# In a seven-product pair the low part of the loaded blocks is made behind the fourth sum

## The chip, the cores and the metric

The kernel runs on one core of a Trainium2 chip. The metric is the device time of one execution in microseconds; the median of three runs of the kernel before is 911.48 us (911.47 to 912.15). The engines are called as the profile calls them: PE (matmul) with PEld (its weight loads), DVE (vector), ACT (scalar), POOL, and SP, whose queue issues the loads.

## The reference

One layer of a decoder trunk on 256 tokens of width 2048, cut to what matters here:

```python
h = rmsnorm(x, norm_g)
h, gate = adaln(h, c, ada_w, ada_b)
proj = jnp.einsum('bsd,de->bse', h, w_in)          # 2048 -> 4 * 4096
b_gate, c_gate, v, g = jnp.split(proj, 4, axis=-1)
u = causal_depthwise_conv(c_gate * v, conv_w)
y = b_gate * u * jax.nn.silu(g)
y = jnp.einsum('bse,ed->bsd', y, w_out)            # 4096 -> 2048
x = x + gate[:, None, :] * y
return rmsnorm(x, final_g)
```

The change lies in the second product, `y` (256 x 4096) by `w_out` (4096 x 2048).

## The kernel before

**Numbers in two parts.** All products are of fp32 numbers, which PE multiplies in a reduced form. So each operand is split: a high part, a cast to `fp32r` on ACT, and a low part, the operand minus its high part, on DVE. A product then is three matmuls (`triple`): high by high, high by low, low by high.

**The stages.** First the norm and the modulation, then the first product, one half of the channels in four chunks and the other in eight pairs of channel tiles (matmuls of line 471, up to about 730 us), then the second product: the first 1024 output columns at once (731 to 816 us), and the other 1024 in two stages of 512 (816 to 903 us). All of its matmuls are line 695.

**The stage of the change** walks through 16 pairs of channel tiles in the order `0, 1, 10, 2, 11, 3, 12, 4, 13, 5, 14, 6, 15, 7, 8, 9`. For each pair the SP queue loads a 1 MiB block of `w_out` (`raw_o`, line 684), 128 partitions by four blocks of 512: two rows of tiles by two halves of columns. An ordinary pair casts it (ACT, line 341, `hi<-raw_o`), takes its low part (DVE, line 346, `lo<-raw_o`) and makes 2 x 2 x 2 products of three matmuls, 24 matmuls, into the PSUM tiles `wide` (`mm_w`).

Pairs 10 to 15 are pairs of seven products: with sums of the token tiles (`forms`, the profile's `form`, made in the stage before) and sums of the blocks of `w_out`, seven products take the place of eight, 21 matmuls in place of 24. From the middle of the stage ordinary pairs and these take turns, and one of each is called a round below. In `seven` the four loaded blocks are `b[:, 0]` to `b[:, 3]`:

- line 720, DVE: the first and the second sum, `b1 - b0` and `b2 - b0` (`sums_o`)
- line 721, ACT: the high part of blocks 1 to 3 (`hi<-raw_o`, 128x1536)
- line 722, DVE: the third sum, block 2 plus the first sum
- line 723, DVE: the fourth sum, block 3 minus the third sum
- line 724, DVE: the low part of blocks 1 to 3
- line 725: the high part (ACT, line 341, `hi<-sums_o`) and the low part (DVE, line 346, `lo<-sums_o`) of the four sums together

Then follow the products: lines 730 to 732 by blocks 1, 3 and 2 as loaded, and lines 733 to 736 by the four sums. The first of these products goes into the PSUM tile `p1`; it, `p6` and `p75` are the profile's `mm`.

**Buffers.** There are three buffers of each kind. A round uses the three `lo` buffers for the ordinary load, the load of the pair of seven and the sums, so the load of the next pair of seven goes into the buffer of the last one, as soon as the last reader of that block is done. The three `hi` buffers hold the three high parts of a round: the cast of the next ordinary block waits until PE has used the last one.

**Order.** Each engine runs its queue in order. What order the instructions of a queue have is worked out when the program is built, from the dependences between them and from durations that the builder assumes; it need not be that of the source. `tc.add_manual_dep(a, b, after, ...)` adds a dependence without a wait: on the same engine, `a` comes behind `b` in the queue. In the trace of before, line 724 stands in front of line 722 in five of the six pairs (DVE: 720, 724, 722, 723), and between 722 and 723 in the pair at 746 us.

Of the kernel before, what the change touches and what calls it, by code (L numbers as in the profile page):

```python
# [8 lines left out]
F32 = mybir.dt.float32  # L9
F32R = mybir.dt.float32r  # L10
AF = mybir.ActivationFunctionType
ALU = mybir.AluOpType
# [105 lines left out]
def short_conv_layer(ctx: ExitStack, tc: tile.TileContext, x, c, norm_g, ada_w, ada_b, w_in, conv_w, w_out, final_g, out):  # L118
    nc = tc.nc
# [25 lines left out]
    def w_tile(kind, name, dtype=F32, i=None):  # L145

        if i is None:
            i = nth[kind] % 3
            nth[kind] += 1
        return wpool.tile([P, SLOT], dtype, tag=f"{kind}{i}", name=name, bufs=1)  # L150
# [12 lines left out]
    after = mybir.DependencyInfo(mybir.DependencyClass.NoSync, mybir.DependencyReason.DATA)  # L163
# [111 lines left out]
    for t in range(TT):  # L275
        for dh in range(2):
# [3 lines left out]
            else:  # L280
                nc.vector.scalar_tensor_tensor(
                    out=junk[:, t], in0=xt[t][dh], scalar=1.0, in1=xt[t][dh], op0=ALU.mult, op1=ALU.mult,
# [50 lines left out]
    def hi_tile():  # L333
        return w_tile("hi", "hi", F32R)

    def lo_tile(lo_tag="lo"):
        return w_tile(lo_tag, "lo", F32R)
# [23 lines left out]
    def split(raw, n, lo_tag="lo"):  # L361

        return split_lo(raw, n, split_hi(raw, n), lo_tag)
# [64 lines left out]
    sums = {}  # L428
# [139 lines left out]
    def gate(dc):  # L568
        return gates[dc // 2][:, dc % 2, :]
# [119 lines left out]
    def y_parts(ct, t):  # L689
        return [ys[ct // 2][:, ct % 2, h, t * P : (t + 1) * P] for h in range(2)]  # L690

    def triple(dst, y, hi, lo, opens=False, ends=False):

        for i, (a, b) in enumerate(((0, hi), (0, lo), (1, hi))):
            nc.tensor.matmul(dst, y[a], b, start=opens and i == 0, stop=ends and i == 2, skip_group_check=True)  # L695
# [17 lines left out]
    def seven(j, raw):  # L713


        opens, last = j == SEVEN[0], j == SEVEN[-1]
        sums = w_tile("lo", "sums_o")
        hi, lo = hi_tile(), lo_tile("raw")
        b, s, bh, bl = (v.rearrange("p (b f) -> p b f", f=W) for v in (raw, sums, hi, lo))
        nc.vector.tensor_tensor(out=s[:, 0:2], in0=b[:, 1:3], in1=b[:, 0:1].to_broadcast([P, 2, W]), op=ALU.subtract)  # L720
        nc.scalar.copy(bh[:, 1:4], b[:, 1:4])
        nc.vector.tensor_tensor(out=s[:, 2], in0=b[:, 2], in1=s[:, 0], op=ALU.add)
        nc.vector.tensor_tensor(out=s[:, 3], in0=b[:, 3], in1=s[:, 2], op=ALU.subtract)
        nc.vector.tensor_tensor(out=bl[:, 1:4], in0=b[:, 1:4], in1=bh[:, 1:4].bitcast(F32), op=ALU.subtract)
        sh, sl = (v.rearrange("p (b f) -> p b f", f=W) for v in split(sums, SLOT, "raw"))

        def f(i):
            return [forms[j][h][:, i] for h in range(2)]

        triple(p1, y_parts(2 * j, 0), bh[:, 1], bl[:, 1], opens, last)  # L730
        triple(wide[0][:, 1], y_parts(2 * j + 1, 0), bh[:, 3], bl[:, 3])
        triple(wide[0][:, 0], f(3), bh[:, 2], bl[:, 2])
        triple(p75[:, 0], f(2), sh[:, 1], sl[:, 1], opens, last)
        triple(p75[:, 1], f(0), sh[:, 0], sl[:, 0], opens, last)
        triple(p6, f(1), sh[:, 2], sl[:, 2], opens, last)
        triple(wide[1][:, 1], y_parts(2 * j + 1, 1), sh[:, 3], sl[:, 3])
# [12 lines left out]
    for n, j in enumerate(order):  # L749
        raw = w_tile("lo" if n else "raw", "raw_o")  # L750
        load_o(raw, 2 * j, 2, 0, 2 * W)
        load_ends(n - 4)
        if j in SEVEN:
            seven(j, raw)
            if j == SEVEN[-1]:
                gather()
            continue
        hi, lo = split(raw, SLOT, "raw")
        for t in range(TT):
            for k in range(2):  # L760
                for d in range(2):
                    o = slice((k * 2 + d) * W, (k * 2 + d + 1) * W)
                    triple(
                        wide[t][:, d], y_parts(2 * j + k, t), hi[:, o], lo[:, o],
                        n == 0 and k == 0, j == order[-1] and k == 1,
                    )
# [24 lines left out]
    for dc in range(2, 4):  # L791
# [16 lines left out]
        for ep in range(n_ep):  # L808
# [3 lines left out]
            if dc == 3:  # L812
# [3 lines left out]
                    out=raw3, in0=raw3, in1=gate(dc).unsqueeze(1).to_broadcast([P, EP, W]), op=ALU.mult  # L816
# [45 lines left out]
```

## Time and profile before

| | us |
|---|---|
| median of three runs | 911.48 |
| the profiled execution | 911.95 |
| its span | 910.2 |
| PE busy | 894.2 |
| DVE busy | 653.5 |
| ACT busy | 476.1 |
| the six DVE instructions of line 724, together | 10.5 |

The 1.75 us between the profiled execution and its span lie around the span. A group or a timeline row reads: engine, line, operation, `out<-in` by the program's names, shapes, count; in square brackets stands how long the engine was idle before it and what ended that. PE runs matmuls back to back, so that a row of a matmul is longer than the distance to the next one; distances are what counts. A weight load (PEld) carries the wait of its matmul.

### The profile page before, as it was taken

To read this page: it belongs to the slowest core of one execution; us is meant where nothing else is said; L and a number is where in the kernel's file an instruction comes from. 1 tells how busy PE (TensorE), PEld (TensorE's weight loads), DVE (VectorE), ACT (ScalarE), POOL (GpSimd) and SP (SyncE) were. 2 spreads that over 40 slices of the span, in tenths; PEclk is the share of its full clock that TensorE was granted. 3 is DMA by queue.
4 is the path that set the end of the run, shared out by engine and by line. 5 is a ranking of instruction groups with operands and counts; after the bars stand their busy time and mean duration, and the time that the engine had idled before them with its cause. 6 is when DMAs were issued, how large, how long until landed. Compare 5 with 4: busy or idle time off the path is not lost.

```text
span 910.2 us, 16272 instructions
## 1 busy us (share of the span) xinstructions
PE 894.2 (98%) x7029; PEld 854.7 (94%) x7029; DVE 653.5 (72%) x647; ACT 476.1 (52%) x422; POOL 0.7 (0%) x6
## 2 busy tenths in 40 slices
PE   6999999999999999999999999999999999999996
PEld 4999999999999999999999999999999987788885
DVE  4889899889888886665555686555555577887882
ACT  6768866665558765643333434343444335544343
POOL 0000000000000000000000000000000000000000
PEclk9999999999999999999999999999999999999998
DMA  9999999999998686676666887656666486685542
GB/s 313 367 371 349 364 309 365 346 370 359 345 327 282 184 301 189 189 241 202 202 186 186 259 273 231 201 185 194 185 193 197 137 307 191 209 293 185 185 138 93
DMA packets 159656, 227.65 MB, mean 250 GB/s; under 512 B 5680, under 2 KB 104160, under 8 KB 159200
## 3 DMA queue, kind: packets, MB, share of 16 engines
q1 hardware_dynamic: 159456, 226.56, 75.7%
q8 instruction: 55, 0.90, 0.4%
q14 instruction: 17, 0.14, 0.0%
q10 hardware_dynamic: 128, 0.04, 0.0%
HBM read 224.49 MB, written 2.10 MB: 249 GB/s over the span
## 4 chain that ended last, share of the span: by engine, by line
PE 98%; ACT 1%; DMA 1%; ACTq 0%; issue 0%; DVE 0%
PE mm_b L471 38%; PE mm_s L471 38%; PE mm_o L695 10%; PE mm_w L695 7%; PE mm L695 2%; PE tp_idle L258 1%; DMA rows<-in_ada_b_dram 1%; PE sum L380 1%; PE ps_gate L596 0%; PE tp_g L461 0%; PE tp_x L310 0%; ACT hi L341 0%; ACT acc L492 0%; ACT hT L327 0%; ACT mm_s L504 0%; ACT big L787 0%
## 5 line engine op out<-in xcount | busy, mean ns | idle before, releaser
L471 PE MATMUL mm_s<-hT,hi 128*128 128x256 f32 x2048 | 350.4, 277 | 0.1
L471 PE MATMUL mm_b<-hT,hi 128*128 128x256 f32 x2048 | 349.4, 276 | 0.0
L471 PEld LDWEIGHTS mm_s<-hT,hi 128*128 128x128 f32 x2048 | 308.5, 188 | 1.0 <-ACT hT L327 0.3
L471 PEld LDWEIGHTS mm_b<-hT,hi 128*128 128x128 f32 x2048 | 308.2, 188 | 0.5 <-issue 0.5
L471 PE MATMUL mm_b<-hT,lo 128*128 128x256 f32 x1024 | 282.6, 276 | 0.0
L471 PE MATMUL mm_s<-hT,lo 128*128 128x256 f32 x1024 | 282.2, 277 | 0.0
L346 DVE TENSOR_TENSOR lo<-raw,hi 128x2048 fp32r<-128x2048 f32 (+1 forms) x66 | 148.0, 2243 | 113.6 <-ACT hi L341 113.2
L341 ACT CAST hi<-raw 128x2048 fp32r<-128x2048 f32 (+1 forms) x66 | 123.7, 1874 | 193.9 <-PE mm_b L471 152.6
L471 PEld LDWEIGHTS mm_b<-hT,lo 128*128 128x128 f32 x1024 | 192.2, 188 | 0.5 <-issue 0.5
L471 PEld LDWEIGHTS mm_s<-hT,lo 128*128 128x128 f32 x1024 | 191.7, 188 | 0.3 <-DVE lo L346 0.2
L346 DVE TENSOR_TENSOR lo<-raw_s,hi 128x2048 fp32r<-128x2048 f32 (+1 forms) x80 | 147.6, 1850 | 32.8 <-ACT hi L341 32.0
L341 ACT CAST hi<-raw_s 128x2048 fp32r<-128x2048 f32 (+1 forms) x80 | 124.0, 1559 | 72.9 <-PE mm_s L471 59.6
L454 DVE SCALAR_TENSOR_TENSOR gv<-at,silu_c,gv 128x512 f32<-128x512 f32 x105 | 78.6, 749 | 6.3 <-DMA at<-in_ada_w_dram 4.5
L341 ACT CAST hi<-raw_o 128x2048 fp32r<-128x2048 f32 x26 | 49.6, 1906 | 60.6 <-PE mm_o L695 36.6
L695 PE MATMUL mm_o<-hi,y 128*128 128x512 f32 x256 | 78.7, 389 | 0.0
L346 DVE TENSOR_TENSOR lo<-raw_o,hi 128x2048 fp32r<-128x2048 f32 x26 | 59.5, 2290 | 24.2 <-ACT hi L341 24.1
L492 ACT COPY acc<-mm_s 128x1024 f32<-128x1024 f32 x54 | 54.6, 1012 | 34.7 <-PE mm_s L471 34.7
L695 PE MATMUL mm_w<-hi,y 128*128 128x512 f32 x184 | 58.2, 390 | 0.0
L695 PEld LDWEIGHTS mm_o<-hi,y 128*128 128x128 f32 x256 | 48.0, 188 | 9.9
L695 PE MATMUL mm_o<-lo,y 128*128 128x512 f32 x128 | 49.5, 389 | 0.0
L593 DVE SCALAR_TENSOR_TENSOR gacc<-at_g,silu_c,gacc 128x512 f32<-128x512 f32 x60 | 45.0, 749 | 5.6 <-DMA at_g<-in_ada_w_dram 4.6
L695 PEld LDWEIGHTS mm_w<-hi,y 128*128 128x128 f32 x184 | 34.5, 188 | 7.7 <-ACT hi L341 0.2
(142 smaller groups left out, 512.6 us busy)
## 6 DMA issues: line engine op xcount, KB each, us to landing
raw<-in_sc_w_in_dram SPq DMA_DIRECT2D x64, 1024.0 KB, 5.6
raw_s<-in_sc_w_in_dram SPq DMA_DIRECT2D x47, 1024.0 KB, 8.5
raw_o<-in_sc_w_out_dram SPq DMA_DIRECT2D x32, 1024.0 KB, 5.1
at<-in_ada_w_dram SPq DMA_DIRECT2D x114, 256.0 KB, 8.4
raw_s<-in_sc_w_in_dram SPq DMA_DIRECT2D x33, 512.0 KB, 6.9
at_g<-in_ada_w_dram SPq DMA_DIRECT2D x32, 512.0 KB, 7.6
at<-in_ada_w_dram SPq DMA_DIRECT2D x6, 512.0 KB, 9.4
x<-in_x_dram SPq DMA_DIRECT2D x4, 512.0 KB, 6.1
```

The lines of the kernel that those rows point to most:

```text
L258: nc.tensor.matmul(tp_idle, ident, ones[:, 0:1].to_broadcast([P, 512]), start=True, stop=True)
L341: nc.scalar.copy(hi[:, :n], raw[:, :n])
L346: nc.vector.tensor_tensor(out=lo[:, :n], in0=raw[:, :n], in1=hi[:, :n].bitcast(F32), op=ALU.subtract)
L380: nc.tensor.matmul(sums0[:, o * P : (o + 1) * P], rows[:, o // NK0, (o % NK0) * P : (o % NK0 + 1) * P], col.to_broadcast([P, P]), start=k ...
L454: nc.vector.scalar_tensor_tensor(out=gv, in0=at4[:, i], scalar=c_k, in1=gv, op0=ALU.mult, op1=ALU.add)
L471: mm = last_mm[0] = nc.tensor.matmul(dst, w, h[k], start=begins and left, stop=ends, skip_group_check=True)
L492: nc.scalar.copy(acc[ch, q], bank)
L593: nc.vector.scalar_tensor_tensor(out=ga, in0=at3[:, i, :], scalar=s, in1=ga, op0=ALU.mult, op1=ALU.add)
L695: nc.tensor.matmul(dst, y[a], b, start=opens and i == 0, stop=ends and i == 2, skip_group_check=True)
```

## The change

Line 724, the low part of the loaded blocks, is given a dependence without a wait on line 723, the fourth sum. Both are DVE instructions, so 724 comes behind 723 in DVE's queue. Nothing else in the source is changed.

```diff
@@ -720,8 +720,9 @@
         nc.vector.tensor_tensor(out=s[:, 0:2], in0=b[:, 1:3], in1=b[:, 0:1].to_broadcast([P, 2, W]), op=ALU.subtract)
         nc.scalar.copy(bh[:, 1:4], b[:, 1:4])
         nc.vector.tensor_tensor(out=s[:, 2], in0=b[:, 2], in1=s[:, 0], op=ALU.add)
-        nc.vector.tensor_tensor(out=s[:, 3], in0=b[:, 3], in1=s[:, 2], op=ALU.subtract)
-        nc.vector.tensor_tensor(out=bl[:, 1:4], in0=b[:, 1:4], in1=bh[:, 1:4].bitcast(F32), op=ALU.subtract)
+        all_sums = nc.vector.tensor_tensor(out=s[:, 3], in0=b[:, 3], in1=s[:, 2], op=ALU.subtract)
+        low = nc.vector.tensor_tensor(out=bl[:, 1:4], in0=b[:, 1:4], in1=bh[:, 1:4].bitcast(F32), op=ALU.subtract)
+        tc.add_manual_dep(low.ins, all_sums.ins.name, after, reason="the sums' cast runs beside the low part")
         sh, sl = (v.rearrange("p (b f) -> p b f", f=W) for v in split(sums, SLOT, "raw"))
```

## The prediction

> **What bounds the kernel now.** I read the page first, for the engine that sets the end.
>
> ```profile
> span 910.2 us, 16272 instructions
> PE 894.2 (98%) x7029; PEld 854.7 (94%) x7029; DVE 653.5 (72%) x647; ACT 476.1 (52%) x422; POOL 0.7 (0%) x6
> PE 98%; ACT 1%; DMA 1%; ACTq 0%; issue 0%; DVE 0%
> raw_o<-in_sc_w_out_dram SPq DMA_DIRECT2D x32, 1024.0 KB, 5.1
> ```
>
> PE carries 98% of the chain of waits, so DVE work counts only where PE has to wait for it. Six of the last sixteen blocks go through the edited function, between 731 and 797 us. The chain of waits in order of time shows whether PE loses anything there (start, length, line, number of matmuls):
>
> ```profile
> 754.84 1.60 PE mm L695 x7
> ...
> 757.12 0.30 PE mm L695
> 757.42 5.23 PE mm_w L695 x23
> ...
> 765.17 0.03 issue
> 765.20 1.89 PE mm L695 x7
> ...
> 767.76 0.38 PE mm L695
> ...
> 775.88 1.88 PE mm L695 x7
> ...
> 778.45 0.39 PE mm L695
> ...
> 786.57 1.87 PE mm L695 x7
> ...
> 789.12 0.36 PE mm L695
> ...
> 797.23 1.89 PE mm L695 x7
> 799.12 11.60 PE mm_w L695 x51
> ...
> 815.93 86.83 PE mm_o L695 x383
> ```
>
> An undisturbed matmul here takes 5.23/23 = 0.227 us, and so does the whole end (86.83/383 = 0.227): behind 799 us PE loses nothing. Two kinds of piece are too long. Seven matmuls should take 1.59, and take 1.60 once and then 1.89, 1.88, 1.87, 1.89: 0.30+0.29+0.28+0.30 = 1.17 us, with the 0.03 of issue 1.20. A single one should take 0.23 and takes 0.30, 0.38, 0.39, 0.36: 0.07+0.15+0.16+0.13 = 0.51. Together **1.7 us**, all that I find to win there. The weight loads of one round say who is late:
>
> ```profile
> 762.26 0.19 PEld L695 LDWEIGHTS mm<-lo,y 128*128 128x128 f32 x1
> ...
> 765.20 0.19 PEld L695 LDWEIGHTS mm<-lo,form 128*128 128x128 f32 x1 [0.34 <-DVE lo L346]
> ...
> 767.64 0.19 PEld L695 LDWEIGHTS mm<-hi,y 128*128 128x128 f32 x1 [0.30 <-ACT hi L721]
> ```
>
> The long groups of seven begin with the first product by the low part of the sums (L346), the long single ones are the first product of the cast block (L721). Behind both stands the DVE queue, whose timeline over one round is
>
> ```profile
> 762.85 2.29 DVE L346 TENSOR_TENSOR lo<-sums_o,hi 128x2048 fp32r<-128x2048 f32 x1 [2.05 <-ACT hi L341]
> 765.06 2.29 DVE L346 TENSOR_TENSOR lo<-raw_o,hi 128x2048 fp32r<-128x2048 f32 x1
> 767.26 1.22 DVE L720 TENSOR_TENSOR sums_o<-raw_o 128x1024 f32<-128x1024 f32 x1
> 768.40 1.75 DVE L724 TENSOR_TENSOR lo<-raw_o,hi 128x1536 fp32r<-128x1536 f32 x1
> 770.07 0.69 DVE L722 TENSOR_TENSOR sums_o<-raw_o,sums_o 128x512 f32<-128x512 f32 x1
> 770.79 0.69 DVE L723 TENSOR_TENSOR sums_o<-raw_o,sums_o 128x512 f32<-128x512 f32 x1
> 773.52 2.29 DVE L346 TENSOR_TENSOR lo<-sums_o,hi 128x2048 fp32r<-128x2048 f32 x1 [2.05 <-ACT hi L341]
> ```
>
> and ACT's, with an earlier and a later row that are needed below:
>
> ```profile
> 741.76 1.91 ACT L341 CAST hi<-raw_o 128x2048 fp32r<-128x2048 f32 x1 [2.50 <-issue]
> ...
> 762.72 1.90 ACT L341 CAST hi<-raw_o 128x2048 fp32r<-128x2048 f32 x1
> 766.11 1.48 ACT L721 CAST hi<-raw_o 128x1536 fp32r<-128x1536 f32 x1 [1.49 <-DMA raw_o<-in_sc_w_out_dram]
> 771.59 1.91 ACT L341 CAST hi<-sums_o 128x2048 fp32r<-128x2048 f32 x1 [4.00 <-DVE sums_o L723]
> 776.81 1.48 ACT L721 CAST hi<-raw_o 128x1536 fp32r<-128x1536 f32 x1 [1.51 <-DMA raw_o<-in_sc_w_out_dram]
> ```
>
> A round (one ordinary pair and one of seven products) takes 773.52 − 762.85 = 10.67 us. PE has 24 + 21 = 45 matmuls in it, 45 × 0.227 = 10.2. So in this stage the DVE queue sets the pace: six operations, then 2.05 us in which it waits for ACT's cast of the sums, and that cast waited 4.00 us for the fourth sum (L723), in front of which L724 stands. PE enters the stage with work ahead, is caught up at 757 us and loses about 0.45 in each round after that.
>
> **The change part by part.** No instruction is added or removed; the same six L724 go from in front of L722 (in front of L723 in one pair) to behind L723. Prices of the new neighbours come from the pair in which the trace happens to have L722 right behind L720, and the place of L724 one round earlier is shown beside them:
>
> ```profile
> 745.91 1.22 DVE L720 TENSOR_TENSOR sums_o<-raw_o 128x1024 f32<-128x1024 f32 x1
> 747.17 0.69 DVE L722 TENSOR_TENSOR sums_o<-raw_o,sums_o 128x512 f32<-128x512 f32 x1
> 747.77 1.75 DVE L724 TENSOR_TENSOR lo<-raw_o,hi 128x1536 fp32r<-128x1536 f32 x1
> ...
> 757.72 1.75 DVE L724 TENSOR_TENSOR lo<-raw_o,hi 128x1536 fp32r<-128x1536 f32 x1
> ```
>
> *The sums.* From L720's start to L723's end it was 770.79 + 0.69 − 767.26 = 4.22 us. It becomes 1.26 (L722 needs L720's result: 745.91 to 747.17) + 0.72 (770.07 to 770.79) + 0.69 = 2.67. The sums' cast, and with it their low part, comes **1.55 us earlier**; the largest lateness to cover was 0.30. The first kind of wait goes: −1.20.
>
> *DVE's round.* 2.21 + 2.20 + 1.26 + 0.72 + 0.69 to the end of L723, 0.11 until the cast starts (770.79 + 0.69 = 771.48, then 771.59), 1.91 of cast and 0.02 to the next L346 (773.52): 9.1 us, with L724's 1.75 inside the cast's 1.91. That is under PE's 10.2, so the DVE queue no longer sets the pace. Without this cover (if the cast were not running then) L724 would cost its 1.67 back and the round be 10.7 again.
>
> *The low part of the loaded block.* It was done 1.13 + 1.75 = 2.9 us after L720's start and is now done 1.26 + 0.72 + 0.60 (747.17 to 747.77) + 1.75 = 4.3 after it: 1.45 later. Who waits: PE's first product by it, loaded at 762.26, while L724 ended at 757.72 + 1.75 = 759.47. That leaves 2.8 us, and still about 1.3 after the shift: nothing. Queued behind L724 is now the sums' low part, which waits for the cast longer than L724 lasts: nothing either.
>
> *The load of the next block.* The buffer of the loaded block was free after L723, now after L724; both times that is all three of L722 to L724 behind L720 (4.22 against 4.33): 0.1 later against L720. It matters through a loop over two rounds, because L721, of which PE already waits, waits for that load. PE's last use of an ordinary block's high part and the latency to ACT are here:
>
> ```profile
> 741.29 0.39 PE L695 MATMUL mm_w<-hi,y 128*128 128x512 f32 x1
> ...
> 772.76 0.61 PE L695 MATMUL mm_w<-hi,y 128*128 128x512 f32 x2
> ```
>
> PE ends at 741.68 and ACT starts at 741.76: 0.08. The loop: ordinary cast 1.90, to its low part 0.02, from that to L720 2.20, L722 1.26, L723 0.72, L724 0.60 and 1.75, free buffer to start of L721 5.33 (771.48 to 776.81), L721 1.48, to PE 0.05 (767.59 to 767.64), from that product to the end of the first matmul of the pair at 772.76 773.15 − 767.64 = 5.51, to ACT 0.08: 20.9 us, 10.45 a round. This is longer than PE's 10.2. So **if PE's queue keeps its order**, only 10.67 − 10.45 = 0.22 of each of the four rounds from 757 to 797 us is won, 0.9 us in all, and L721 becomes the bound.
>
> The Trainium skill (DMA: Bandwidth & Descriptors, section Anatomy of one DMA — SWDGE (gpsimd) path) gives 2.0 us plus the bytes at 436 GB/s, an estimate of 4.4 us for 1 MiB; it is fitted to another issue path than this kernel's. By it the loop would be 20.9 − 0.8 = 20.1, under two of PE's rounds (20.4), and this wait would go with the old queue order too. The trace has 5.1 to landing for this very transfer, and that is what I used.
>
> *PE's order.* Each queue's order is worked out when the kernel is built, from the dependences and the builder's own durations, and the trace shows only the result for the old ones: the first product of the cast block (767.64) stands ahead of most of the ordinary pair's 24 products (the 23 `mm_w` matmuls that follow it in the chain), as a filler while their low part was still missing. What is not to be seen is where it stands after the edit. Lower bound of the stage's gain 0.9 (same place), upper bound 1.7 (behind the ordinary products, where L721 has some 22 × 0.227 = 5.0 us more). I take the upper one as likelier: with L724 last, that block is loaded 1.55 later against the sums' cast than before, while the ordinary low part no longer queues behind a late one, so there is less to fill and the filler comes later.
>
> *Sum:* −1.20 − 0.51 = −1.7. The profiled execution is 911.95 with its span of 910.2; it becomes 910.25 with a span of 908.5. It lies 0.47 above the median of the runs, 911.48, from which I subtract the same: **909.8 us**.
>
> **The rivals.**
>
> *Same queue, new bound (B).* Gain 0.9: 910.6. For it: the filler's place and the load's 5.33 us come from rows. Against it: the reasons just given for a later place.
>
> *Nothing comes of it (C).* PE's first product by L724's result moves at least 1.3 us (6 matmuls) ahead and waits there instead, or L724 isn't where the edit puts it: about 911.4. Against it: the row at 762.26 with its 2.8 us, and in the pair at 745.91 L724 has already stood behind L722 with no wait behind it, though PE still had work ahead then.
>
> *The filler moves ahead (D), slower.* If the builder places the cast block's first product earlier in PE's queue, the loop grows by 0.227 for each place, 0.11 a round. At two places it eats B's gain (0.22); from there the kernel is slower than before. Ten places ahead, right behind the first high product of the ordinary pair, it would be 1.13 − 0.22 = 0.9 a round, 3.6 over four rounds: 915.1. For it: it is a filler now, with PE waiting 0.30 for it. Against it: fewer gaps are left to fill.
>
> *More than the stage holds (E).* Another queue order behind 799 us wins something too; the chain shows no loss there up to 902 us: 909.4 at best.
>
> **How the numbers follow.** A 0.52 (its own range 909.5 to 910.1), B 0.20, C 0.12, D 0.13, E 0.03. The range from 909.4 to 911.6 holds A, B, C and E nearly whole and the mildest of D, a little over 0.8. What a measurement of this kernel can tell from no change is about 0.2%, 1.8 us, so faster means below 909.66: 0.22 of A's 0.52 and E, 0.25. Slower means above 913.3: D without its mild part, 0.12. The rest, 0.63, is within.
>
> **What would show it.** Right: in every pair the order on DVE is L720, L722, L723, L724; L723 to the sums' cast stays near 0.1 us; L724 lies beside that cast; weight loads no longer wait for L346; groups of seven last 1.59; rounds take 10.2 us. B shows in weight loads that wait longer for L721, in rounds near 10.45. C shows in loads that wait for L724, D in waits for L721 of a microsecond and rounds over 10.7. I am wrong in the cause if the rounds shrink to 10.2 and the end of PE's work does not move, or if anything changes ahead of 733 us.

## The result, and the profile after

| | before | after |
|---|---|---|
| median of 19 runs each, on one chip (us) | 911.89 (911.24 to 915.29) | 910.21 (909.54 to 911.04) |
| ratio to before, 95% interval | | 0.998 (0.9973 to 0.9987) |
| span of the profiled execution (us) | 910.2 | 909.3 |

The kernel became 1.68 us faster, 1.2 to 2.5 by the interval; 1.7 was predicted. Since PE sets the end, I compare the stage on PE itself, from its first `mm_w` matmul to the first of the 384 `mm_o` matmuls of the end. The chain of waits of before in order of time (start, length, line, matmuls), with its rows that were not shown yet:

```profile
730.79 10.89 PE mm_w L695 x48
...
764.69 0.48 PE mm_w L695 x2
...
777.76 0.70 PE mm_w L695 x3
...
810.72 0.23 PE mm_o L695
```

and the same view of the changed kernel:

```profile
731.28 10.89 PE mm_w L695 x48
...
755.10 1.59 PE mm L695 x7
...
765.30 1.59 PE mm L695 x7
766.88 5.89 PE mm_w L695 x26
772.78 0.23 PE mm L695
...
775.50 1.59 PE mm L695 x7
...
785.70 1.59 PE mm L695 x7
...
795.91 1.60 PE mm L695 x7
797.51 16.80 PE mm_w L695 x74
814.31 87.05 PE mm_o L695 x384
```

The rounds are 10.20 us each (755.10, 765.30, 775.50, 785.70): 45 matmuls and nothing lost. The stage takes 814.31 − 731.28 = 83.03 us. Before it took 815.93 − 730.79 = 85.14, of which 0.23 is the one `mm_o` matmul that ran inside it, so 84.91. The change is worth **1.88 us** there. Both kinds of long pieces are gone: every group of seven takes 1.59 or 1.60, every single one 0.23. That was 1.71; of the other 0.17 some hundredths stand in short groups such as the two of before that are shown above (0.48 and 0.70 in place of 0.45 and 0.68).

The spans of the two profiles differ by 0.9 only. In that of the change, the slowest of its 19 runs (911.04), the stage begins 0.49 later (731.28 against 730.79; between 729.4 and 731.3 in all the profiles below, though PE's order is the same up to there). And behind PE's last matmul there are 7.9 us (901.36 to 909.3) in place of 7.4 (902.76 to 910.2). This end is longer in the profiles of e1, e4, e6 and e7 below too, by 0.2 to 0.4, and not in those of e2, e3 and e5. Why is open.

Why PE no longer waits, DVE's timeline over one round says:

```profile
761.33 2.29 DVE L346 TENSOR_TENSOR lo<-sums_o,hi 128x2048 fp32r<-128x2048 f32 x1 [0.38 <-ACT hi L341]
764.60 2.29 DVE L346 TENSOR_TENSOR lo<-raw_o,hi 128x2048 fp32r<-128x2048 f32 x1 [0.98 <-ACT hi L341]
766.81 1.22 DVE L720 TENSOR_TENSOR sums_o<-raw_o 128x1024 f32<-128x1024 f32 x1
768.06 0.69 DVE L722 TENSOR_TENSOR sums_o<-raw_o,sums_o 128x512 f32<-128x512 f32 x1
768.78 0.69 DVE L723 TENSOR_TENSOR sums_o<-raw_o,sums_o 128x512 f32<-128x512 f32 x1
769.39 1.75 DVE L724 TENSOR_TENSOR lo<-raw_o,hi 128x1536 fp32r<-128x1536 f32 x1
771.52 2.29 DVE L346 TENSOR_TENSOR lo<-sums_o,hi 128x2048 fp32r<-128x2048 f32 x1 [0.38 <-ACT hi L341]
```

and ACT's:

```profile
766.23 1.48 ACT L721 CAST hi<-raw_o 128x1536 fp32r<-128x1536 f32 x1 [1.66 <-DMA raw_o<-in_sc_w_out_dram]
769.59 1.91 ACT L341 CAST hi<-sums_o 128x2048 fp32r<-128x2048 f32 x1 [1.88 <-DVE sums_o L723]
772.86 1.91 ACT L341 CAST hi<-raw_o 128x2048 fp32r<-128x2048 f32 x1 [1.36 <-PE mm_w L695]
777.21 1.48 ACT L721 CAST hi<-raw_o 128x1536 fp32r<-128x1536 f32 x1 [2.44 <-DMA raw_o<-in_sc_w_out_dram]
```

The sums take 768.78 + 0.69 − 766.81 = 2.66 us. Their cast starts 0.12 behind L723 (769.47 to 769.59), L724 runs beside it, and DVE now waits 0.38 and 0.98 in a round in place of 2.05. The bound has moved: the ordinary cast waits for PE's release of its buffer (1.36), so DVE and ACT go at PE's pace of 10.20.

The cast at 777.21 is late, 6.07 us behind L724's end (771.14) where 5.33 was reckoned, and still PE does not wait for it. The first product of that cast block is loaded at 782.59, 3.9 us behind the cast's end (778.69), without a wait. The weight loads of the round before show the new order: the first row is the cast block's first product, the second the first product by L724's result:

```profile
772.39 0.19 PEld L695 LDWEIGHTS mm<-hi,y 128*128 128x128 f32 x1
...
772.84 0.19 PEld L695 LDWEIGHTS mm<-lo,y 128*128 128x128 f32 x1
```

The first product of the cast block, at 767.64 in the old order with 23 matmuls behind it, now stands right behind the ordinary pair's last matmul. A line-by-line comparison of PE's order says the same of pairs 12 to 15:

```
@@ -4239,6 +4238,5 @@
 L695 MATMUL mm_w<-hi,y_4467 128x512
-L695 MATMUL mm_w<-hi,y_3623 128x512
-L695 MATMUL mm_8263<-hi,y_4468 128x512
+L695 MATMUL mm_w<-hi,y_3623 128x512 x2
...
@@ -4257,4 +4255,5 @@
 L695 MATMUL mm_w<-hi,y_3623 128x512
+L695 MATMUL mm_8263<-hi,y_4468 128x512
 L695 MATMUL mm_w<-hi,y_4468 128x512
```

So the edit of one DVE instruction changed two queues: DVE's as written, and PE's because the builder worked it out anew. (The ordinary pair's first high product, too, no longer stands ahead of the products by the sums' low part. ACT's and SP's orders are as before.) Which of the two brings the gain, or both, is the question for the experiments.

### The profile page after: what moved, and what is told of

It is laid out like the page before. It is cut to its first block, busy times and chain, and to the rows that moved or that the text cites. A ratio compares the mean times of both kernels' runs of the same rounds, so it can differ in the third digit from the quotient of the medians.

```text
span 909.3 us, 16270 instructions
## 1 busy us (share of the span) xinstructions
PE 892.8 (98%) x7029; PEld 855.6 (94%) x7029; DVE 654.7 (72%) x647; ACT 476.4 (52%) x422; POOL 0.7 (0%) x6
## 4 chain that ended last, share of the span: by engine, by line
PE 97%; ACT 1%; DMA 1%; ACTq 0%; issue 0%; DVE 0%
PE mm_b L471 38%; PE mm_s L471 38%; PE mm_o L695 10%; PE mm_w L695 7%; PE mm L695 2%; PE tp_idle L258 1%; DMA rows<-in_ada_b_dram 1%; PE sum L380 1%; PE ps_gate L596 0%; PE tp_g L461 0%; PE tp_x L310 0%; ACT hi L341 0%; ACT acc L492 0%; ACT hT L327 0%; ACT mm_s L504 0%; ACT big L788 0%
## 5 line engine op out<-in xcount | busy, mean ns | idle before, releaser
L346 DVE TENSOR_TENSOR lo<-raw,hi 128x2048 fp32r<-128x2048 f32 (+1 forms) x66 | 147.9, 2243 | 113.4 <-ACT hi L341 113.0
L346 DVE TENSOR_TENSOR lo<-raw_s,hi 128x2048 fp32r<-128x2048 f32 (+1 forms) x80 | 147.5, 1849 | 33.0 <-ACT hi L341 31.6
L346 DVE TENSOR_TENSOR lo<-raw_o,hi 128x2048 fp32r<-128x2048 f32 x26 | 59.5, 2290 | 29.8 <-ACT hi L341 29.7
```

Source lines behind the costliest of these rows:

```text
L346: nc.vector.tensor_tensor(out=lo[:, :n], in0=raw[:, :n], in1=hi[:, :n].bitcast(F32), op=ALU.subtract)
```

## The experiments

All seven kernels make the whole output. Each was timed against the kernel before on the same chip (median of before 911.65 us for the first four, 911.7 for the other three). An edit moves line numbers by two to eight, so the old L721 is L726 in some rows, and so on. *Opener* is my name for the cast block's first product; `seven` gets no other edit than those shown or named. The stage length is the one of the section above, from one profile each.

| kernel | DVE order | opener on PE | median us | ratio (95%) | stage us |
|---|---|---|---|---|---|
| before | L724 first | behind 2 of the ordinary pair's 24 | 911.89 | | 84.91 |
| the change | L724 last | behind 24 | 910.21 | 0.998 (0.9973 to 0.9987) | 83.03 |
| e1 | L724 last | behind 2, pairs 12 to 15 | 912.09 | 1.0008 (0.9998 to 1.0017) | 84.62 |
| e2 | L724 first | behind 24 | 911.94 | 1.0004 (0.9995 to 1.0013) | 84.85 |
| e3 | ahead of the fourth sum | left to the builder | 911.7 | 1.0 (0.9992 to 1.0009) | 84.87 |
| e6 | L724 last | as e1, but pair 14 as the change | 911.46 | 0.9997 (0.9988 to 1.0006) | 83.73 |
| e7 | L724 last | behind 12 | 910.32 | 0.9982 (0.9973 to 0.9991) | 83.03 |
| e4 | L724 last | ten places ahead of before | 917.9 | 1.0072 (1.0058 to 1.0085) | |
| e5 | behind the sums' low part | left to the builder | 930.17 | 1.0207 (1.0193 to 1.0221) | |

### The two halves alone: DVE's order with PE's old one (e1), PE's order with DVE's old one (e2)

e1 keeps the change and puts the opener back near its old place (24 matmuls in `pair`; the helper is used in all that follow but e3 and e5):

```diff
+    def put_behind(late, first):
+        tc.add_manual_dep(late.ins, first.ins.name, after, reason="order on PE")
...
+    def place(j, pair, opener7, seven_before):
+        if j >= 12:
+            for i, mm in enumerate(pair):
+                if i in (0, 12):
+                    put_behind(opener7, mm)
+                else:
+                    put_behind(mm, opener7)
```

> The change, with the first product of the cast block put back to its old place on PE in pairs 12 to 15 (ahead of all but two of the ordinary pair's 24 matmuls). Theory (the change has two parts, DVE's order and PE's, and with the old place the loop over two rounds through the load sets the pace): no wait for the sums' low part is left, the waits for the cast of the loaded blocks grow to about 0.5 us in two rounds, rounds of 10.45 us on average, 0.9 us faster than before, that is 0.7 slower than the change. Rival (the waits are independent of each other, so the one for the cast stays at its old 0.15 a round): rounds of 10.35 us each, 1.2 us faster than before. Second rival (PE's order is without effect): as the change, 1.7 faster than before.

It came to 912.09 us, no gain (0.2 at most by the interval), where rival B had 0.9. The rest of PE's order is that of the change: the ordinary pair's first high product stands behind the products by the sums' low part. The weight loads with a wait, in its stretch from 755 to 790 us, are no longer those for the sums' low part; all three are for the cast of loaded blocks:

```profile
756.64 0.19 PEld L697 LDWEIGHTS mm<-hi,y 128*128 128x128 f32 x1 [0.36 <-ACT hi L726]
766.90 0.19 PEld L697 LDWEIGHTS mm<-hi,y 128*128 128x128 f32 x1 [0.20 <-ACT hi L726]
778.38 0.19 PEld L697 LDWEIGHTS mm<-hi,y 128*128 128x128 f32 x1 [1.41 <-ACT hi L726]
```

The third is the large one, and the chain that ends there shows the loop step by step:

```profile
762.23 1.91 ACT hi L341
...
764.16 1.16 DVE lo L346
...
766.37 1.23 DVE sums_o L725
...
767.62 0.70 DVE sums_o L727
...
768.35 0.69 DVE sums_o L728
769.04 1.68 DVE lo L729
...
770.74 6.02 DMA raw_o<-in_sc_w_out_dram
...
776.86 1.48 ACT hi L726
...
778.38 0.50 PE mm L697
```

It is the loop that the prediction added up, with one length different: from the free buffer to the cast it takes 6.14 us here (770.72 to 776.86), where 5.33 was reckoned; the load itself takes 6.02. From one ordinary cast to the second next the trace has 751.57 to 772.49 = 20.92 us (20.9 predicted), and 762.23 to 783.99 = 21.76 for the one with the long load. The mechanism of B holds, its price does not: a loop that is the bound passes each late load on to PE. In this profile the stage is 0.29 us shorter than before; it is the profile of the fastest of the eleven runs (911.50), and what the others lose beyond it was not profiled.

e2 forces the old order on DVE and the new one on PE:

```diff
-        nc.vector.tensor_tensor(out=s[:, 2], in0=b[:, 2], in1=s[:, 0], op=ALU.add)
+        third = nc.vector.tensor_tensor(out=s[:, 2], in0=b[:, 2], in1=s[:, 0], op=ALU.add)
...
-        tc.add_manual_dep(low.ins, all_sums.ins.name, after, reason="the sums' cast runs beside the low part")
+        tc.add_manual_dep(third.ins, low.ins.name, after, reason="the low part first")
...
+        for mm in pair:
+            put_behind(opener7, mm)
```

> Before's order on DVE (the low part of the loaded blocks in front of the third and the fourth sum), with PE's order of the change: the first product of the cast block behind the ordinary pair. Theory (DVE's round of 10.67 us sets the pace, and what PE no longer loses at the cast it loses at the sums' low part): rounds stay at 10.67, the wait for the cast is gone, the one for the sums' low part grows from 0.29 to about 0.45 a round, time as before within 0.3 us. Rival (the two kinds of wait add up): the 0.5 us at the cast are won, 0.5 faster than before, rounds of 10.5.

911.94 us, no gain either. Only the opener has moved here; the ordinary pair's first high product is still ahead of the products by the sums' low part, as before. Its weight loads with a wait, one round of them, and the groups of seven in its chain:

```profile
775.60 0.19 PEld L697 LDWEIGHTS mm_w<-hi,y 128*128 128x128 f32 x1 [0.28 <-ACT hi L341]
776.12 0.19 PEld L697 LDWEIGHTS mm<-lo,form 128*128 128x128 f32 x1 [0.33 <-DVE lo L346]
```

```profile
765.45 1.88 PE mm L697 x7
776.13 1.89 PE mm L697 x7
786.80 1.87 PE mm L697 x7
```

Rounds are 10.68 and 10.67 us, as before. The wait for the cast of the loaded block is gone, and the 0.5 us that stood beside it is not won: it turned into a wait for the ordinary cast. I had expected it to be added to the wait for L346, which stayed at 0.33; in sum it is the same, because DVE's round of 10.67 was still the bound.

So each half alone wins nothing that can be measured, and both together 1.7. What the move of the ordinary pair's first high product does by itself was not tried.

### The place on DVE: ahead of the fourth sum (e3), behind the sums' low part (e5)

```diff
-        tc.add_manual_dep(low.ins, all_sums.ins.name, after, reason="the sums' cast runs beside the low part")
+        tc.add_manual_dep(low.ins, third.ins.name, after, reason="behind the third sum")
+        tc.add_manual_dep(all_sums.ins, low.ins.name, after, reason="ahead of the fourth sum")
```

> The low part of the loaded blocks between the third and the fourth sum in all six pairs: behind one sum more than before, but still ahead of what the sums' cast waits for. Theory (only the time from the first sums to the end of the fourth counts): 1.26 + 0.60 + 1.67 + 0.69 = 4.22 us as before, rounds of 10.67, time as before within 0.3 us. Rival (each sum that it is moved behind brings its part): about half of the change, 0.8 us faster than before.

911.7 us, as before: as long as L724 is ahead of the last sum, the cast waits for it and DVE's round stays. The builder left PE's order as it was before in all matmuls. One place further back than the change is e5:

```diff
-        sh, sl = (v.rearrange("p (b f) -> p b f", f=W) for v in split(sums, SLOT, "raw"))
+        sums_hi = split_hi(sums, SLOT)
+        sums_lo = lo_tile("raw")
+        low_sums = nc.vector.tensor_tensor(out=sums_lo, in0=sums, in1=sums_hi.bitcast(F32), op=ALU.subtract)
+        tc.add_manual_dep(low.ins, low_sums.ins.name, after, reason="behind the low part of the sums")
+        sh, sl = (v.rearrange("p (b f) -> p b f", f=W) for v in (sums_hi, sums_lo))
```

> The low part of the loaded blocks one step later still, behind the low part of the sums. Theory (the load of the next pair of seven starts when the last reader of the block is done, so a loop over one round runs from the first sums through the low part and the load back to the first sums): 1.26 + 0.72 + 0.69 + 0.11 + 1.91 + 0.02 + 2.21 + 1.75 + 5.33 = 14.0 us a round against PE's 10.2, four rounds, some 15 us slower than the change, more where PE's clock drops after its long gaps (eight matmuls at 0.45 us in the run with the product far ahead), 925 to 932. Rival (only DVE's own queue counts, 2.21 + 1.67 + 2.20 + 1.26 + 0.72 + 0.69 + 0.11 + 1.91 + 0.02 = 10.8 us a round): 2.4 us slower than the change, 912.5.

930.17 us, 18.5 slower. Its DVE timeline:

```profile
761.01 1.23 DVE L720 TENSOR_TENSOR sums_o<-raw_o 128x1024 f32<-128x1024 f32 x1 [3.07 <-DMA raw_o<-in_sc_w_out_dram]
...
767.92 1.75 DVE L724 TENSOR_TENSOR lo<-raw_o,hi 128x1536 fp32r<-128x1536 f32 x1
...
775.05 1.23 DVE L720 TENSOR_TENSOR sums_o<-raw_o 128x1024 f32<-128x1024 f32 x1 [3.17 <-DMA raw_o<-in_sc_w_out_dram]
```

L724 holds the buffer of the loaded block. Behind the cast and the low part of the sums it frees it so late that load, sums, cast, low part and L724 become a loop over one round: 775.05 − 761.01 = 14.04 us. The place that the change takes, behind the sums and beside their cast, is the only one of the four that costs neither the cast nor the load.

### The place on PE: ten places ahead (e4), only one pair (e6), half way (e7)

e4 puts the opener right behind the first high product of the ordinary pair, ahead of the rest of the pair before, and holds DVE's order of the change (in `seven`, line 720 is put behind the ordinary pair's low part):

```diff
+            put_behind(opener7, pair[0])
+            for mm in pair[1:]:
+                put_behind(mm, opener7)
+            for i, mm in enumerate(seven_before[9:]):
+                if i not in (0, 6, 9):
+                    put_behind(mm, opener7)
+                else:
+                    put_behind(opener7, mm)
```

> The change, with the first product of the cast block ten places further ahead on PE than it stood before (right behind the ordinary pair's first high product), in pairs 12 to 15; DVE's order is that of the change. Theory (loop over two rounds through the load, 20.9 us at the old place plus 0.227 for each place): 23.2 us, rounds of 11.6, four of them 1.4 us over PE's 10.2, so 5 to 6 us slower than the change and 3 to 4 slower than before, with PE waiting over a microsecond for the cast of the loaded blocks. Rival (the loads have slack and the cast comes when DVE's order allows): at most a wait of 0.5 us a round, no slower than before.

917.9 us (917.0 to 919.53), 6.3 slower than before. All weight loads of the opener wait:

```profile
755.58 0.29 PEld L699 LDWEIGHTS mm<-hi,y 128*128 128x128 f32 x1 [2.60 <-ACT hi L729]
768.29 0.19 PEld L699 LDWEIGHTS mm<-hi,y 128*128 128x128 f32 x1 [1.11 <-ACT hi L729]
781.35 0.19 PEld L699 LDWEIGHTS mm<-hi,y 128*128 128x128 f32 x1 [2.97 <-ACT hi L729]
794.15 0.19 PEld L699 LDWEIGHTS mm<-hi,y 128*128 128x128 f32 x1 [1.11 <-ACT hi L729]
```

Together 7.8 us. The direction of rival D is right and its price too low; 3.6 had been worked out for ten places. Two pieces more can be seen in the profile. The load in pair 14 again took long: its cast came 6.38 us behind the release (773.45 to 779.83), 1.05 more than in the sum. And behind the two long gaps PE ran at half its clock for a while, as the granted clock says (window, its length, busy time of PE, PEld, DVE, ACT and POOL, PEclk, DMA share, GB/s):

```profile
753.00:755.50 2.50, 0.40 (x2) 0.00 (x0) 2.50 (x2) 1.45 (x1) 0.00 (x0) 0.98 0.16 61
755.50:757.50 2.00, 1.92 (x5) 1.54 (x6) 1.93 (x4) 0.03 (x1) 0.00 (x0) 0.50 0.78 190
...
768.00:770.00 2.00, 1.71 (x7) 1.42 (x8) 2.00 (x2) 0.24 (x1) 0.00 (x0) 1.00 0.00 0
...
783.30:785.30 2.00, 2.00 (x6) 1.54 (x5) 1.35 (x1) 0.37 (x1) 0.00 (x0) 0.50 0.76 311
```

PE did 0.40 us of work in 753.00 to 755.50, then eight matmuls took 3.59 (755.58 to 759.17, the next piece of the chain) in place of 1.82; behind the third wait 33 matmuls took 9.41 in place of 7.49. The stage is 93.50 us in this profile, 10.5 longer than in the change; about 5.6 of it are the loop's as it was reckoned (four rounds of 11.6 in place of 10.2), 1.05 the late load and 3.7 the half clock. The profiled run is the slowest of the four, with a mean clock of 0.993; the other three (917.0 to 918.0) had 0.998 and 0.999, like before, so the clock is not what made those slow. What their waits consist of was not profiled.

e6 is e1 with pair 14, the one with the long load, left at its new place:

```diff
-        if j >= 12:
+        if j >= 12 and j != 14:
```

> The change with the first product of the cast block at its old place in pairs 12, 13 and 15, and at its new one in pair 14, the one whose load took 6.0 us from issue to landing where the others took 5.0 to 5.3. Theory (the loop of 20.9 us over two rounds holds, and what made the run with all four at the old place no faster than before was the 0.85 us of that one load): no long wait in pair 14, waits of 0.2 to 0.5 us in the other three, 0.8 us faster than before. Rival (the old place itself costs what DVE's order wins): as before within 0.3 us.

911.46 us, 0.24 less than before with an interval from −1.1 to +0.5. By time alone the two expectations cannot be told apart. Its profile agrees with the theory: no wait in pair 14, and one in each of the three others, 0.33, 0.19 and, the last,

```profile
788.36 0.19 PEld L697 LDWEIGHTS mm<-hi,y 128*128 128x128 f32 x1 [0.53 <-ACT hi L726]
```

with a stage of 83.73 us, 1.18 below before. The run of this profile is the median one (911.46) all the same: its stage began 0.26 later than before's (731.05), and the end behind PE's last matmul is 0.42 longer, 7.86 us (901.84 to 909.7). So about 0.5 of the 1.18 is left in the span. Why that end is longer is open.

e7 puts the opener half way, behind 12 of the 24:

```diff
+                if i < 12:
+                    put_behind(opener7, mm)
+                else:
+                    put_behind(mm, opener7)
```

> The change with the first product of the cast block half way, behind the first twelve matmuls of the ordinary pair, ten places behind its old place and twelve ahead of its new one, in pairs 12 to 15. Theory: the loop over two rounds is 20.9 less ten times 0.227, 18.6 us, 19.5 with the slow load, both under PE's 20.4: no wait for the cast is left and the time is that of the change, 1.7 faster than before. Rival (the loop is mis-sized by more than 0.9 us): waits for the cast remain in the traces, and a part of the 1.7 is missing.

910.32 us, the time of the change, with its stage of 83.03. No weight load waits, though the cast of a loaded block in pair 14 waited longer for its load here than in the change (2.44) or e1 (2.46):

```profile
777.08 1.48 ACT L726 CAST hi<-raw_o 128x1536 fp32r<-128x1536 f32 x1 [3.02 <-DMA raw_o<-in_sc_w_out_dram]
```

Ten places (behind 12 in place of 2), 10 × 0.227 = 2.3 us, are enough to take up a load that is late by 1 us. No version that I tried beats the change by what can be told apart.

## Why the prediction was right

**The two waits (−1.20 and −0.51): right.** Both kinds are gone from the chain; the stage won 1.88 against 1.71, the whole kernel 1.68. That the 1.68 falls so near to 1.7 is in part luck: the stage won 0.2 more, the end behind PE's last matmul was 0.5 longer in the profile, and the interval is 1.2 to 2.5.

**The sums and the cast: right.** L720 to the end of L723 is 2.66 us (2.67 predicted), the cast begins 0.12 behind (0.11), and L724 lies beside it.

**DVE's round: right as a bound.** 9.1 us had been worked out for it; it is not seen as such, because PE's 10.20 now sets the pace and DVE waits 0.38 + 0.98 in a round. Without the 0.98, the wait that was not there before, the round would be 9.2. (Without the cover it would have been 9.12 + 1.67 = 10.8, not the 10.7 written there.)

**The low part comes later at no cost: right.** L724 ends at 771.14, PE loads the first weights for its product at 772.84: 1.7 us left, 1.3 predicted. Rival C fell.

**PE's order: right, and it was the step that decided.** I had put it at 0.52 against 0.20 with an argument from the builder's side (less to fill, so the filler comes later). The opener did move behind the ordinary pair. e1 shows what it was worth: with the old place the gain is gone. That argument itself was not tested: no run shows why the builder moved the opener, only that it left it in place with L724 ahead of the last sum (e3). At a chance of 0.52 the deciding step was little more than an even bet.

**Rival B: mechanism right, price wrong.** Its loop of 20.9 us is in the trace of e1 (20.92). It was valued at 0.9 us with the 5.33 of one load of before; in e1 the load of pair 14 took 0.8 more, and B's time would have been about the 911.4 of rival C, not 910.6. My range held both. The sum of 20.1 us that stands beside it takes off 0.8, where the 5.1 to landing that is named there gives 0.7; e1, where PE waits at the opener in three rounds, speaks for 20.9.

**Rival D: too cheap.** 0.11 us a round for each place gave 3.6 for ten places; e4 lost 6.3. The formula held the load at its usual length and the clock at full speed, and its profile shows neither. In the three runs at full clock a part of the loss stays open.

**Nothing ahead of the stage: right. Nothing behind it: right for PE alone.** PE's order is unchanged up to 754 us, and its matmuls of the end take what they took (87.05/384 = 0.227). The prediction put nothing down for what comes behind the last of them; that was 0.5 us longer in the profile.

## What to carry to other kernels

When two queues both run just over the pace of a third, a repair of one alone shows nothing: look for the next bound under the wait you remove, and look at what the builder does to the other queues' order. Price an instruction that frees a buffer by the loop in which it stands (release, load, cast, next use), and give that loop slack against the longest load in the trace rather than the usual one. If a product can stand anywhere in a stretch of independent ones, put it where its input may be a microsecond late.

## What the runs showed of the hardware

**A load that is late in some orders.** The load for pair 14, issued at about 771 us, took 5.9 us to landing in the changed kernel, where the median of the 32 is 5.2. In the other profiles of kernels with L724 last (e1, e4, e6, e7) it took 6.0 to 6.5, in those with L724 ahead (before, e2, e3) 5.0 to 5.4, and 5.4 also in e5, where L724 is later still. The DMA view of the changed kernel from 770 to 777 us, in 40 slices:

```profile
GB/s 421 421 374 468 374 374 398 234 70 0 0 0 140 140 0 164 117 117 140 398 374 421 421 421 421 398 398 398 421 421 398 211 47 23 23 23 23 23 0 0
...
q8 instruction: 1, 0.02, 0.9%
```

The last seven slices with traffic, 1.2 us, move 23 to 211 GB/s where the ones ahead move some 400: most of the transfer is done, a small part lags. One fetch of instructions (the second row) shares the engines in that stretch. Such a fetch lies near the same load in the kernels with a short one as well, so it is no more than a suspect; it was not tested.

**The clock fell after gaps of 2.2 and 2.6 us.** In the profile of e4 PE stood from 753.40 to 755.58 and from 778.80 to 781.35. Behind both the clock was granted at 0.50 (the windows above); it stayed at 1.00 behind the gaps of 0.7 us at 768 and 794 us. The other three runs of e4 show no fall in their mean clock (0.998 and 0.999); all four of e5 have 0.989 or 0.990. The Trainium skill (TensorE: Matmul & The Clock Gate, section HAM oscillation — how this bites in real kernels) gives as the rule that gaps over about 3.4 us bring it to half; here shorter ones did. The halving itself agrees.
